# Weight splits recorded one preparation later, attention handed out more often, in a one-core encoder layer

## The chip, the cores and the metric

The kernel runs on one core of one Trainium2 chip. It uses five engines: PE (matrix products; PEld is its loading of stationary operands), DVE and ACT (elementwise work), POOL (here only the issue of DMAs that add) and SP (the issue of all other DMAs). The metric is the time of one execution in device microseconds (us). The kernel before took 2253.76 us, the median of three runs between 2248.48 and 2257.56.

## The reference

The layer is applied to a prompt of 512 tokens and to a sample of 1024 tokens, with the same weights and a model width of 2048. Cut to what matters:

```python
def mixer_layer(x, ...):
    h = rms_norm(x, norm_g)
    z = h @ w_in                      # 2048 -> 5632 columns
    c_val, c_glu, c_gate, q, k, v, a_gate = split(z)
    q, k = rope(q), rope(k)           # 8 query heads, 2 key/value heads of 128
    conv = (silu(layer_norm(depthwise31(c_val * sigmoid(c_glu)) + b)) @ w_pw) * silu(c_gate)
    attn = banded_sink_attention(q, k, v, sink) * silu(a_gate)   # window 128, blocks of 128
    return x + concat([conv, attn]) @ w_out
# the encoder is one such layer and a final rms_norm
```

All of it is float32. A product on PE runs on float32r operands, so each float32 operand is split in two (a rounded high part, made by ACT, and the remainder, made by DVE), and three matmuls (high-high, high-low, low-high) stand for one.

## The kernel before, in words

**Stages.** The sample is projected first, by units. A `Unit` makes two column tiles of 128 for all 1024 tokens over half of the 2048 rows of `w_in`, as a two-by-two block product with seven products in place of eight. So a unit has seven steps of 12 matmuls of 512 columns, 84 in all, and needs four weight operands (made by `make0` to `make3`), one for steps 0 and 1, one for 2 and 3, one for 4 and 5, one for 6. There are 44 units in four stages: 8 convolution units on the first half of the rows, 8 on the second, then 14 units of the remaining columns on the second half, and the same 14 on the first half. Three of the four stages begin with a pair of units whose steps alternate (the second of them has `side` set). Then the prompt is projected by 44 jobs of 48 matmuls (`Job`, line 482; the weight is split again, or its low part is fetched as the units stored it). After that come three tails (`Post`): the sample's first and second 512 tokens, and the prompt. Each is the pointwise product (8 jobs of 24 matmuls) and the output product (16 jobs of 48; the last tail makes it in another form, line 1228).

**The weight splits.** `w_prep(upto)` makes the operands in order up to (not including) number `upto`: ACT copies the raw weight tile into the high half of an `hl` tile (line 350), DVE subtracts for the low half (line 351), and for `make1` to `make3` DVE first forms sums of raw blocks (line 136). There are three `hl` buffers and three `raw` buffers. While step or job with operand `i` is recorded, the kernel before calls `w_prep(i + NHL)` with NHL = 3 behind its first products, so operands up to `i + 2` are made there; a call `w_prep(i + 1)` stands ahead of each step. Each operand made also starts the load of raw tiles up to two numbers ahead.

**What sets the order.** The code records instructions; a scheduler then gives each engine one fixed order, by the order of recording and by priority (weight splits, evacuations and what follows them are recorded as urgent). On the chip every engine goes through its order one by one, and an instruction that waits holds up what is behind it on its engine.

**Evacuation of a unit.** After each step `tap` reads a bank of sums: ACT copies (line 208) or DVE adds the bank to an earlier copy (line 210). Four of the seven taps complete a tile of 128 columns by 512 tokens: the taps of steps 1, 4 and 5 (DVE) and 6 (ACT). On the second half of the rows that a column group sees, POOL then issues a DMA that adds the stored sums of the first half into the tile in place (`add_into`, line 341), and an entry is put in a list, `later`, with the count LANDING = 4. Each recorded step calls `turn_over`, which takes one off each count, and at zero records `done` for the tile behind the DVE and ACT instructions recorded last: the multiplication by the rms factor (lines 739 and 741 with a sigmoid between, 745 for the product with the gate, 754 for gates and values) or the rotation of a query or key (lines 806 to 809), all on DVE. Bank `a` is one running sum over steps 0, 2, 4 and 6, so step 6 cannot start before DVE has read the bank behind step 4. This second half is the convolution units of the second stage (8 units) and all units of the fourth (14): 88 added tiles.

**Lanes.** Work that has no fixed place is put in lanes (convolution taps, line 778; attention; preparations). After each group of three matmuls the code calls `tick(648 ns)`; a lane gets a credit of that time times its rate, and records pieces of work, each with a cost in the code, while its credit is positive. From the start of the prompt's projection the attention lane has the rate RUSH = 1.2. It holds the sample's two groups of 8 blocks, then the 8 heads of `attention_parts` for the first tail, then the prompt's two groups of 4 blocks. Before the first output product of a tail all 8 heads must be there: `until` records the rest of the lane at once, with no products between. The same is done for the prompt's attention ahead of the last tail's preparation. In the code's costs a block of attention is 38.8 us (35.3 at the ends of a sequence), the keys and values of a group are 22 us (11 for the prompt), a head of `attention_parts` is 6 us.

Of the kernel before, what the change touches and what calls it, by code (L numbers as in the profile page):

```python
# [34 lines left out]
NORM = 2  # L35
SOON = 800
PM = 30
RUSH = 1.2
LANDING = 4
LOAD = 4500  # L40
SPREAD = 3
RATES = (0.4, 0.6, 0.3, 1.0)
# [2 lines left out]
NT, NRAW, NHL = 28, 3, 3  # L45
# [40 lines left out]
class Unit:  # L86
# [82 lines left out]
    def product(self, step, late):  # L169
        e, nc = self.e, self.e.nc  # L170
        p, o = OPERAND[step]
        i = self.at[p]
        e.w_prep(i + 1)
        hl = e.hl[i]
        n = BANK[step]
        if step in FRESH:
            self.bank[n] = e.PS(self.tags[n], [W])
        acc = self.bank[n]
        toks = e.T[SUMS[step]]
        for j in range(HALF):  # L180
            for q, (l, r) in enumerate(((0, 0), (0, 1), (1, 0))):
                nc.tensor.matmul(  # L182
                    acc,
                    hl[:, l, o, j, :],
                    toks[j][:, r],
                    start=step in FRESH and j == 0 and q == 0,
                    stop=step in LAST and j == HALF - 1 and q == 2,
                    skip_group_check=True,
                )
            if j == 0:  # L190
                for fn in late:
                    fn()
                e.w_prep(i + NHL)
                e.turn_over()
            e.tick(3 * MM)
        if step in (1, 3, 5, 6):
            e.hl.pop(i)
        for fn in self.after.get(step, ()):
            fn()
        return [lambda: e.urgently(self.tap, step)]  # L200

    def tap(self, step):
# [8 lines left out]
        if step in (1, 4, 5, 6):  # L211
            part, d = self.part[n[0]][n[1]], self.d.pop(n)
            if self.done:

                e.add_into(d, part)
                e.later.append([LANDING, lambda: self.done(n[0], n[1], d)])
            else:
# [53 lines left out]
class Encoder:  # L271
# [182 lines left out]
    def run(self, items):  # L454

        nc = self.nc
        late = []
        for n, item in enumerate(items):
            for x in item:
                for fn in x.before:  # L460
                    fn()
            if isinstance(item[0], Unit):
                for u in item:
                    u.open()
                for step in range(7):
                    for u in item:
                        late = u.product(step, late)
                continue
            while self.later:
                self.turn_over(True)  # L470
            job = item[0]
            job.acc = [self.acc()]
            nk = len(job.ks)
            for q in range(0, nk, 2 * HALF):
                at = job.at + q // (2 * HALF)
                self.w_prep(at + 1)
                hl = self.hl.pop(at)
                for kk in range(2 * HALF):
                    i = q + kk
                    hi, lo = job.rhs(job.ks[i])  # L480
                    for p, (l, r) in enumerate(((0, hi), (0, lo), (1, hi))):
                        nc.tensor.matmul(  # L482
                            job.acc[0],
                            hl[:, l, kk // HALF, kk % HALF, :],
                            r,
                            start=i == 0 and p == 0,
                            stop=i == nk - 1 and p == 2,
                        )
                    if kk == 0:
                        self.w_prep(at + NHL)  # L490
                        self.turn_over()
                    if i in job.ticks:
                        job.ticks[i]()
                    self.tick(3 * MM)
                    if i == 0:
                        for fn in late:
                            fn()
                        late = []
            late = [lambda job=job: self.urgently(job.evac, job.acc)]
        for fn in late:  # L500
            fn()
# [764 lines left out]
def encoder(ctx, tc, a):  # L1266
# [76 lines left out]
    def pace(unit, rate, lane=e.conv):  # L1343
        unit.before.append(lambda: setattr(lane, "rate", rate))
# [53 lines left out]
    pj[0].before.append(attend)  # L1398
    pace(pj[0], RUSH, e.attn)
    pace(pj[0], RATES[3])  # L1400
# [72 lines left out]
```

## Time and profile before

| | |
|---|---|
| Median of the runs | 2253.76 us (2248.48 to 2257.56) |
| The profiled execution: its own time, its span | 2254.38 us, 2252.5 us |
| PE busy, share of the span | 2159.6 us, 96% |
| DVE busy | 1648.9 us, 73% |
| ACT busy | 965.6 us, 43% |
| POOL busy | 77.0 us, 3% |
| DMA | 400.11 MB, 178 GB/s over the span |
| Mean granted clock of PE | 0.98 |

A row of the profile's tables gives the program line, the engine, the operation and the operands, written tile first, without buffer numbers; then the count, the busy time and the mean of one. In a timeline a row begins with its start and its duration in us, and the bracket at its end is the idle time of the engine just before it, with what ended it. Rows of stretches give the stretch's start and end, its length, the busy time and count of each engine (PE, PEld, DVE, ACT, POOL), then the granted clock of PE, the DMA engines' busy share and GB/s. A busy PE is not a PE at its full rate, because matmuls overlap: the full rate is read from the distance of starts.

### The profile page before, as it was taken

The numbers are of one execution on the slowest core, as the hardware profiler recorded it, in microseconds if no ns is written. First come the engines' busy times: TensorE is split into PE (matmuls) and PEld (weight loads), VectorE is DVE, ScalarE is ACT, GpSimd is POOL, SyncE is SP. The second block draws the span as 40 slices with busy tenths as digits, with TensorE's granted clock in tenths as the row PEclk, the third lists the DMA queues.
The fourth block names the chain that finished last, engine by engine and source line by source line (L and its number), as shares of the span: only waits on it lengthen the run. The fifth ranks groups of instructions, "written<-read, shape, count | busy, mean of one in ns | idle before, by whom it ended". The sixth has DMA issues, their size and how long they took to land.

```text
span 2252.5 us, 26360 instructions
## 1 busy us (share of the span) xinstructions
PE 2159.6 (96%) x9510; PEld 1752.0 (78%) x9510; DVE 1648.9 (73%) x2497; ACT 965.6 (43%) x1484; POOL 77.0 (3%) x92
## 2 busy tenths in 40 slices
PE   6999899999999999899999999996999999999998
PEld 5887777888877787688888888884788777888886
DVE  8657788988898999799986688673663775746343
ACT  5465335333443334433444457443352544623232
POOL 0001110000011111000000000000000000000000
PEclk8999999999999999999999999996999999999999
DMA  8968767754576666855444644443542482447342
GB/s 283 321 221 245 203 168 255 263 178 164 196 202 175 157 164 160 262 176 168 141 140 142 201 139 136 149 143 120 186 154 104 153 286 84 163 136 259 103 131 75
DMA packets 207748, 400.11 MB, mean 178 GB/s; under 512 B 18945, under 2 KB 76673, under 8 KB 207617
## 3 DMA queue, kind: packets, MB, share of 16 engines
q1 hardware_dynamic: 194944, 375.35, 49.5%
q0 software_dynamic: 12672, 23.07, 6.4%
q8 instruction: 74, 1.21, 0.2%
q14 instruction: 58, 0.47, 0.1%
HBM read 294.02 MB, written 104.33 MB: 177 GB/s over the span
## 4 chain that ended last, share of the span: by engine, by line
PE 68%; DVE 6%; DMA 5%; issue 2%; ACT 1%; SPq 0%; POOL 0%; ACTq 0%; DVEq 0%; POOLq 0%
PE a L482 19%; PE c L482 10%; PE b L482 9%; PE a L182 9%; PE c L182 4%; PE pv L921 2%; PE s L889 2%; PE b L182 2%; PE a L1228 2%; PE s L1228 2%; DMA raw<-w_in 1%; PE pt L926 1%; DVE hl L351 1%; DVE f L778 1%; DMA u<-q_d 1%
## 5 line engine op out<-in xcount | busy, mean ns | idle before, releaser
L351 DVE TENSOR_TENSOR hl<-raw,hl 128x1024 fp32r<-128x1024 f32 (+1 forms) x323 | 371.8, 1151 | 248.3 <-ACT hl L350 243.4
L350 ACT ACTIVATE hl<-raw 128x1024 fp32r<-128x1024 f32 (+1 forms) x323 | 323.0, 1000 | 537.0 <-PE a L482 110.5
L482 PE MATMUL a<-t,hl 128*128 128x512 f32 x2112 | 511.9, 392 | 0.0
L182 PE MATMUL a<-t,hl 128*128 128x512 f32 x1968 | 480.9, 396 | 30.0 <-DVE g L210 17.9
L182 PEld LDWEIGHTS a<-t,hl 128*128 128x128 f32 x1968 | 374.5, 191 | 116.9 <-DVE g L210 25.1
L482 PEld LDWEIGHTS a<-t,hl 128*128 128x128 f32 x2112 | 393.4, 188 | 78.5
L778 DVE SCALAR_TENSOR_TENSOR f<-f,c_w_dw,f 128x1024 f32<-128x1024 f32 (+1 forms) x464 | 453.4, 1012 | 1.0 <-ACT f L773 1.0
L482 PE MATMUL b<-t,hl 128*128 128x512 f32 x1056 | 260.0, 395 | 10.7 <-ACT t L350 10.4
L482 PE MATMUL c<-t,hl 128*128 128x512 f32 x1056 | 256.2, 392 | 0.1
L182 PE MATMUL c<-t,hl 128*128 128x512 f32 x984 | 240.9, 392 | 9.7 <-ACT t L350 5.7
L482 PEld LDWEIGHTS b<-t,hl 128*128 128x128 f32 x1056 | 197.3, 189 | 56.8 <-ACT t L350 14.3
L482 PEld LDWEIGHTS c<-t,hl 128*128 128x128 f32 x1056 | 196.4, 188 | 39.4 <-DVE hl L351 0.5
L182 PEld LDWEIGHTS c<-t,hl 128*128 128x128 f32 x984 | 185.0, 188 | 51.6 <-ACT t L350 7.0
L182 PE MATMUL b<-t,hl 128*128 128x512 f32 x492 | 118.5, 389 | 0.0
L136 DVE TENSOR_TENSOR raw<-raw,raw 128x512 f32<-128x512 f32 x123 | 84.6, 688 | 38.6 <-DMA raw<-w_in 28.3
L182 PEld LDWEIGHTS b<-t,hl 128*128 128x128 f32 x492 | 92.3, 188 | 19.1
L208 ACT ACTIVATE u<-a 128x512 f32<-128x512 f32 x66 | 39.4, 597 | 91.8 <-PE a L182 86.9
L921 PE MATMUL pv<-a,t 128*128 128x512 f32 x192 | 71.1, 434 | 4.8 <-ACT a L350 3.9
L1228 PE MATMUL a<-hl,t 128*128 128x512 f32 x192 | 74.7, 390 | 0.0
L889 PE MATMUL s<-t,a 128*128 128x384 f32 (+1 forms) x288 | 61.5, 344 | 11.6 <-ACT a L350 10.0
L903 ACT ACTIVATE p<-p,tiny 128x384 f32<-128x384 f32 (+1 forms) x96 | 54.5, 569 | 38.8 <-DVE tiny L900 38.6
L889 PEld LDWEIGHTS s<-t,a 128*128 128x128 f32 x288 | 49.8, 201 | 23.8 <-ACT a L350 14.1
(242 smaller groups left out, 2139.5 us busy)
## 6 DMA issues: line engine op xcount, KB each, us to landing
raw<-w_in SPq DMA_DIRECT2D x169, 512.0 KB, 4.8
raw<-w_out SPq DMA_DIRECT2D x64, 512.0 KB, 3.9
raw<-w_out SPq DMA_DIRECT2D x64, 256.0 KB, 3.3
raw<-w_pw SPq DMA_DIRECT2D x24, 512.0 KB, 3.5
f<-xT_s SPq DMA_DIRECT2D x38, 256.0 KB, 5.9
f<-x_s SPq DMA_DIRECT2D x16, 512.0 KB, 6.1
f<-x_p SPq DMA_DIRECT2D x13, 512.0 KB, 7.2
g<-part_q POOLq DMA_DIRECT2D x24, 256.0 KB, 4.9
```

What stands on the lines that cost most here:

```text
L136: self.e.nc.vector.tensor_tensor(out, x, y, ALU.subtract)
L182: nc.tensor.matmul(acc, hl[:, l, o, j, :], toks[j][:, r], start=step in FRESH and j == 0 and q == 0, stop=step in LAST and j == HALF - 1 a ...
L208: nc.scalar.activation(self.d[n], bank, AF.Copy)
L350: nc.scalar.activation(hi, x, AF.Copy)
L351: nc.vector.tensor_tensor(lo, x, hi.bitcast(F32), ALU.subtract)
L482: nc.tensor.matmul(job.acc[0], hl[:, l, kk // HALF, kk % HALF, :], r, start=i == 0 and p == 0, stop=i == nk - 1 and p == 2,)
L778: nc.vector.scalar_tensor_tensor(t, h[:, j : j + T], w(j), t, ALU.mult, ALU.add)
L889: nc.tensor.matmul(ps[:, 0:n], qs[:, x, h], k[y][:, keys], start=p == 0, stop=p == 2)
L903: nc.scalar.activation(p[:, 0:n], p[:, 0:n], AF.Exp, bias=nm[:, h : h + 1], accum_out=l[:, h : h + 1])
L921: nc.tensor.matmul(pv, v[x][:, vs], pt[:, y], start=i == 0 and p == 0, stop=i == last and p == 2)
L926: nc.tensor.transpose(tp[:, h], p[:, i * P : (i + 1) * P], e.ident)
L1228: nc.tensor.matmul(acc, self.mix[self.KS[i]][:, m, b * P : (b + 1) * P], part[l].rearrange("p a b -> p (a b)"), start=i == 0 and p == 0, s ...
```

## The change

Three things are changed. Weight splits are recorded one operand less far ahead (`NHL - 1` in place of `NHL`), and in units only in every second step (the odd ones for a `side` unit, the even ones for the others). LANDING goes from 4 to 3, so that `done` is recorded one step earlier. RUSH goes from 1.2 to 1.45. The number of matmuls, splits, taps and DMAs is the same; behind line 192 the lines of the changed kernel are two higher.

```diff
-RUSH = 1.2
-LANDING = 4
+RUSH = 1.45
+LANDING = 3
...
@@ Unit.product
             if j == 0:
                 for fn in late:
                     fn()
-                e.w_prep(i + NHL)
+
+                if step % 2 == self.side:
+                    e.w_prep(i + NHL - 1)
                 e.turn_over()
             e.tick(3 * MM)
...
@@ Encoder.run
                     if kk == 0:
-                        self.w_prep(at + NHL)
+                        self.w_prep(at + NHL - 1)
                         self.turn_over()
```

How the order moves is seen at two places. The first is DVE in a query unit of the fourth stage. `g_5675<-a` is the tap of step 4, `g_5654<-c` the tap of step 5, a wait on DMASW is a wait for an added tile; the order before:

```order
L210 TENSOR_TENSOR g_5675<-a_5573,g_5675 128x512 [waits DMAHW3_49,PE_49]
L806 TENSOR_TENSOR u_5694<-u_5599,f_5003 64x512 [waits DMASW0_49]
L807 TENSOR_TENSOR u_5694<-u_5599,f_5003 64x512
L136 TENSOR_TENSOR raw_5584<-raw_5584,raw_5715 128x512 [waits DVE_49]
L808 TENSOR_TENSOR u_5599<-u_5599,f_5002 128x512 [waits DVE_49]
L210 TENSOR_TENSOR g_5654<-c_5650,g_5654 128x512 [waits DMAHW6_49,PE_49]
L809 TENSOR_TENSOR u_5599<-u_5599,u_5694 128x512 [waits DVE_49]
L351 TENSOR_TENSOR hl_5718<-raw_5715,hl_5718 128x1024 [waits Activation_49]
L778 SCALAR_TENSOR_TENSOR f_5610<-f_5485,c_w_dw,f_5610 128x1024
L351 TENSOR_TENSOR hl_5738<-raw_5631,hl_5738 128x1024 [waits PE_49,Activation_49]
L778 SCALAR_TENSOR_TENSOR f_5609<-f_5485,c_w_dw,f_5609 128x1024
L754 TENSOR_TENSOR g_5675<-g_5675,f_1667 128x512 [waits DMASW1_49]
```

Ten rows stand between the tap of step 4 and line 754, which takes the tile after its addition. The same unit on DVE in the changed kernel, from the tap of step 4:

```order
L212 TENSOR_TENSOR g_5670<-a_5571,g_5670 128x512 [waits DMAHW6_49,PE_49]
L136 TENSOR_TENSOR raw_5634<-raw_5634,raw_5732 128x512 [waits DVE_49]
L780 SCALAR_TENSOR_TENSOR f_5567<-f_5449,c_w_dw,f_5567 128x1024
L212 TENSOR_TENSOR u_5655<-c_5651,u_5655 128x512 [waits PE_49]
L353 TENSOR_TENSOR hl_5735<-raw_5732,hl_5735 128x1024 [waits Activation_49]
L756 TENSOR_TENSOR g_5670<-g_5670,f_1661 128x512 [waits DMASW1_49]
L780 SCALAR_TENSOR_TENSOR f_5568<-f_5449,c_w_dw,f_5568 128x1024
L756 TENSOR_TENSOR u_5655<-u_5655,f_1661 128x512 [waits DMASW2_49]
```

Four rows are left between the tap of step 4 and line 756 (754 before), three between the tap of step 5 and its line 756. The weight split `hl` that stood ahead of them (with a wait for PE) comes later, and `done` with its DMA wait has moved up. The tap of step 1 and its rotation stand closer as well: before, 12 rows lie between them, now 4:

```order
L212 TENSOR_TENSOR u_5754<-b_5750,u_5754 128x512 [waits DMAHW4_49,PE_49,Activation_49]
L353 TENSOR_TENSOR hl_5817<-raw_5634,hl_5817 128x512 [waits Activation_49]
L780 SCALAR_TENSOR_TENSOR f_5567<-f_5449,c_w_dw,f_5567 128x1024
L136 TENSOR_TENSOR raw_5876<-raw_5820,raw_5778 128x512 [waits DMAHW7_49,DMAHW1_49,DVE_49]
L136 TENSOR_TENSOR raw_5876<-raw_5820,raw_5876 128x512 [waits DVE_49]
L808 TENSOR_TENSOR u_5822<-u_5754,f_4999 64x512 [waits DMAHW6_49,DMASW4_49]
```

Here line 808 (806 before) waits for the tile that line 212 (210 before) completed, with a split, one convolution tap and two raw sums between.

The second place is PE around the first output product. Before, the last block of the sample's attention (`pt` are transposes, `pv` the product with the values) ends like this, and the output product follows at once:

```order
L921 MATMUL pv_12022<-a_12028,t_1290_9660 128x512 [waits Activation_49]
L921 MATMUL pv_12022<-a_12028,t_1290_9660 128x512 [waits DVE_49]
L921 MATMUL pv_12022<-a_12028,t_1291_9661 128x512
L926 MATMUL pt_12034<-c_ident,p_11989 128x128 [waits PE_49]
L926 MATMUL pt_12034<-c_ident,p_11995 128x128
L926 MATMUL pt_12034<-c_ident,p_12001 128x128
L926 MATMUL pt_12034<-c_ident,p_12007 128x128
L921 MATMUL pv_12022<-a_12039,t_1290_9660 128x512 [waits Activation_49]
L921 MATMUL pv_12022<-a_12039,t_1290_9660 128x512 [waits DVE_49]
L921 MATMUL pv_12022<-a_12039,t_1291_9661 128x512
L482 MATMUL b_12114<-t_1665_12053,hl_11847 128x512 [waits Activation_49]
L482 MATMUL b_12114<-t_1665_12053,hl_11847 128x512 [waits DVE_49]
```

No product of a projection stands between these rows. In the changed kernel the last block of the sample's attention is spread through the prompt's projection (`c` and `a` are its sums, line 484 is 482 before):

```order
L928 MATMUL pt_11653<-c_ident,p_11503 128x128 [waits PE_49]
L928 MATMUL pt_11653<-c_ident,p_11509 128x128
L928 MATMUL pt_11653<-c_ident,p_11529 128x128
L928 MATMUL pt_11653<-c_ident,p_11535 128x128
L484 MATMUL c_11565<-t_909_7018,hl_11472 128x512 x3
L484 MATMUL c_11565<-t_910_7021,hl_11472 128x512 x3
L484 MATMUL c_11565<-t_911_7024,hl_11472 128x512 x3
L484 MATMUL a_11673<-t_886_6915,hl_11621 128x512 x3
L923 MATMUL pv_11630<-a_11658,t_1261_9344 128x512 [waits Activation_49]
L923 MATMUL pv_11630<-a_11658,t_1261_9344 128x512 [waits DVE_49]
L923 MATMUL pv_11630<-a_11658,t_1262_9345 128x512
L484 MATMUL a_11673<-t_887_6918,hl_11621 128x512 x3
```

Between the transposes and the products that need them there are now 12 matmuls of the projection, and the block ends at PE's matmul 6301 in place of 6538.

## The prediction, made before the changed kernel ran

> **What bounds the kernel now.** I read the page first, then stretches cut at the stages, then the timelines where PE waits.
>
> ```profile
> span 2252.5 us, 26360 instructions
> PE 2159.6 (96%) x9510; PEld 1752.0 (78%) x9510; DVE 1648.9 (73%) x2497; ACT 965.6 (43%) x1484; POOL 77.0 (3%) x92
> ```
> ```profile
> 407.17 5.44 PE a L182 x24
> ```
> ```profile
> 180.70:349.70 169.00, 156.63 (x673) 126.91 (x672) 135.46 (x177) 66.68 (x94) 26.93 (x31) 0.98 0.74 203
> 622.60:916.60 294.00, 277.42 (x1194) 225.96 (x1193) 263.25 (x346) 122.35 (x176) 47.97 (x55) 0.98 0.67 178
> 916.60:1528.30 611.70, 608.03 (x2778) 495.96 (x2777) 498.99 (x819) 289.67 (x458) 0.87 (x1) 1.00 0.49 159
> 1528.30:1581.50 53.20, 32.28 (x94) 18.38 (x91) 20.02 (x39) 14.28 (x29) 0.00 (x0) 0.68 0.41 129
> ```
> PE is the bound nearly everywhere. Its full rate is in the chain of waits: 24 matmuls in 5.44 us, so 0.2267 us each and 19.04 us for a unit of 84. By that rate the second stage (8 units, 152.3 us) has lost 16.7 us of its 169.0, and the fourth (14 units, 266.6 us) 27.4 of its 294.0. The prompt's projection, 916.6 to 1528.3, shows PE busy for 608 of 612 us. Then comes a hole: in 53.2 us PE runs 94 matmuls, which need at most 94 x 0.2267 = 21.3 us, and its clock is 0.68. In the fourth stage DVE is busy for 263 of 294 us: there it has next to nothing to spare.
>
> **Part 1: the hole (RUSH).**
>
> ```profile
> 1525.65 2.89 PE L482 MATMUL a<-t,hl 128*128 128x512 f32 x12
> 1528.37 0.60 PE L926 MATMUL pt<-c_ident,p 128*128 128x128 f32 x4
> ...
> 1548.48 1.09 PE L926 MATMUL pt<-c_ident,p 128*128 128x128 f32 x4 [3.88 <-DVE p L911]
> ...
> 1562.23 1.95 PE L482 MATMUL b<-t,hl 128*128 128x512 f32 x3 [6.53 <-ACT t L350]
> ```
> These rows of PE's timeline are what `until` recorded at once: the end of the sample's attention and the 8 heads, with nothing of a projection to put between. The credits say why. 44 jobs of 16 groups and 8 of 8 groups, 0.648 each, give 498 us by the first output product. The sample's attention costs 651 and the 8 heads 48, together 699. At 1.2 the lane has 597, so 102 are left; at 1.45 it has 722, and nothing is. The order bears it out (the last block ends 237 matmuls sooner, among products). What moves into the projection is about 20 us of DVE and 14 of ACT; there DVE is busy for 499 and ACT for 290 of 612 us, so it is covered; without that cover it would cost up to those 20 us. Gain: at least 53.2 - 21.3 = 31.9, at most 36, since transposes and scores are shorter than 0.2267; I take 33, as a wait or two stays.
>
> The prompt's attention is due later. Past the hole 218 us of ticks give 261 at 1.2 against its 318, so it is forced too; at 1.45 it has 23 + 316 = 339 and is through.
>
> ```profile
> PE s L889 <- ACT a L350: 8.6, 4, 4.1
> ```
> That is PE's wait for attention operands between 1580 and 2030 us; I take 6 of the 8.6 (bounds 0 and 8.6). Together 39.
>
> **Part 2: the splits recorded later.** The same splits are made. An `hl` tile is free when its last reader is through, and with three buffers that instant does not move; only the place in DVE's and ACT's order does. What is behind an early split waits with it:
>
> ```profile
> DVE hl L351 <- ACT hl L350: 248.8, 153, 6.6
> PE s L182 <- ACT hl L350: 5.2, 1, 5.2
> ```
> ```profile
> L350 ACT ACTIVATE hl<-raw 128x1024 fp32r<-128x1024 f32 (+1 forms) x323 | 323.0, 1000 | 537.0 <-PE a L482 110.5
> L351 DVE TENSOR_TENSOR hl<-raw,hl 128x1024 fp32r<-128x1024 f32 (+1 forms) x323 | 371.8, 1151 | 248.3 <-ACT hl L350 243.4
> L208 ACT ACTIVATE u<-a 128x512 f32<-128x512 f32 x66 | 39.4, 597 | 91.8 <-PE a L182 86.9
> ```
> The first row is DVE's wait for splits over the span (longest 6.6); PE is not held by it except where DVE is full. Its end is worth nothing by itself, since PE's own wait for a split is the second row alone (the first pair of the fourth stage), which goes: 5 us. In the other direction, a unit's operand must be there 24 matmuls (5.4 us) after the one before; a split is 1.0 us on ACT and 1.15 on DVE (the third row, line 208, is the ACT copy of a tap, 0.6 us, for part 3). That holds, unless DVE is late for another reason; bounds +5 and -5, and I take 0, since four additions of that pair now come close on their taps as in part 3.
>
> **Part 3: `done` closer to the DMA it needs (LANDING and the splits).** This is what the order shows on DVE. Durations are those of a unit before, by the distance of starts:
>
> ```profile
> 723.13 1.22 DVE L351 TENSOR_TENSOR hl<-raw,hl 128x1024 fp32r<-128x1024 f32 x1
> 724.27 0.68 DVE L210 TENSOR_TENSOR g<-a,g 128x512 f32<-128x512 f32 x1
> 724.98 0.69 DVE L806 TENSOR_TENSOR u<-u,f 64x512 f32<-64x512 f32 x1
> 725.68 0.68 DVE L807 TENSOR_TENSOR u<-u,f 64x512 f32<-64x512 f32 x1
> 726.40 0.69 DVE L136 TENSOR_TENSOR raw<-raw,raw 128x512 f32<-128x512 f32 x1
> 727.01 0.68 DVE L808 TENSOR_TENSOR u<-u,f 128x512 f32<-128x512 f32 x1
> 727.61 0.68 DVE L210 TENSOR_TENSOR g<-c,g 128x512 f32<-128x512 f32 x1
> 728.21 0.68 DVE L809 TENSOR_TENSOR u<-u,u 128x512 f32<-128x512 f32 x1
> 728.81 1.22 DVE L351 TENSOR_TENSOR hl<-raw,hl 128x1024 fp32r<-128x1024 f32 x1
> 729.94 1.28 DVE L778 SCALAR_TENSOR_TENSOR f<-f,c_w_dw,f 128x1024 f32<-128x1024 f32 x1
> 731.14 1.22 DVE L351 TENSOR_TENSOR hl<-raw,hl 128x1024 fp32r<-128x1024 f32 x1
> 732.27 1.28 DVE L778 SCALAR_TENSOR_TENSOR f<-f,c_w_dw,f 128x1024 f32<-128x1024 f32 x1
> 733.47 0.68 DVE L754 TENSOR_TENSOR g<-g,f 128x512 f32<-128x512 f32 x1
> ```
> ```profile
> 728.70 0.86 POOL L341 DMA_DIRECT2D g<-part_q  x1 [2.27 <-DVE g L210]
> ```
> ```profile
> g<-part_q POOLq DMA_DIRECT2D x1, 256.0 KB, 4.1
> g<-part_q POOLq DMA_DIRECT2D x1, 256.0 KB, 4.8
> g<-part_q POOLq DMA_DIRECT2D x1, 256.0 KB, 5.8
> u<-part_q POOLq DMA_DIRECT2D x1, 256.0 KB, 5.4
> ```
> ```profile
> DMA to landing us min/median/max: 3.8/5.2/9.5
> ```
> A split takes 1.14, a convolution tap 1.20, the two half rotations 0.70 each, every other row 0.6. POOL begins 0.41 us after a tap's end (728.29 to 728.70), and the four additions of one unit (787 to 799 us) land 4.1, 4.8, 5.8 and 5.4 later. Before, the tap of step 4 ends at 724.95 and line 754 begins at 733.47, 8.5 us on: the 4.5 needed are covered. Now the rows between them:
>
> - Tap of step 4 from 0 to 0.65; raw sum, convolution tap and the tap of step 5 to 3.05; a split to 4.2. Its tile is there at 0.65 + 0.41 + 4.1 = 5.15: DVE waits 0.95.
> - Line 754 to 5.75, a tap to 6.95. The tile of step 5 is there at 3.05 + 0.41 + 4.8 = 8.25: 1.3 more. Then 0.6 and a split, 10.0.
> - The tile of step 6: PE may start the step at 0.75, ends at 3.5 (5.1 at half clock), ACT copies to 4.2 to 5.8, POOL and landing 6.2: there at 10.4 to 12.0, wait 0.4 to 2.0, I take 1.2. Rotation (2.6) and the tap of step 1 to 14.45; split, tap and two raw sums to 17.45.
> - That tile is there at 14.45 + 0.41 + 5.4 = 20.25: 2.8. Rotation, raw sum and a split: 24.6, and the next unit's tap of step 4.
>
> So a unit has 18.3 us of DVE work and 6.3 of waits, 24.6 us, where PE needs 19.04: the stage becomes DVE's, and PE waits behind step 4 for bank `a`. The trace before shows once what that looks like:
>
> ```profile
> 254.87 0.69 DVE L739 TENSOR_TENSOR u<-u,f 128x512 f32<-128x512 f32 x1 [3.44 <-DMA u<-part_conv]
> ```
> ```profile
> 264.39 7.70 PE L182 MATMUL a<-t,hl 128*128 128x512 f32 x24 [4.58 <-DVE g L210]
> ```
> One addition late by 3.44 us, and PE stood still for 4.58 soon after, then ran 24 matmuls in 7.70 in place of 5.6, at half clock.
>
> ```profile
> 708.70:871.30 162.60, 156.92 (x673) 127.90 (x672) 0.98 0.62 159
> ```
> The eight query units took 162.6 us, 20.3 each. Now 8 x 24.6 = 197, less 3 that PE's lead at their start absorbs (step 5, 12 matmuls, lies between the tap's end of step 4 and step 6): +31. The stage's other six units took 294.0 - 162.6 = 131.4, 21.9 each. Four of them (keys and values, and the last two) have 16 to 19 us of DVE work by the same durations and get the same waits, about 23.4 each: +6, an estimate. In the second stage a unit has four or five convolution taps, 16.6 to 17.8 us of DVE work by the same durations; three of its four additions are read 2.6 to 3.5 us of work after their taps, and the waits by the same sum are 5.4 (1.8, 0.8, 2.8): 22 to 23.2 us a unit against 169.0 / 8 = 21.1, with seven units so placed and the loss of 254 us kept: +14. Sum +51. Bounds: with every landing at 3.8 the waits are 2.6 a unit, and the sum is +15; nothing below that, as no row shows a shorter landing. With half of them at 7 it is +90.
>
> The Trainium skill has a rule that speaks the other way: by "DMA: Bandwidth & Descriptors", section "Anatomy of one DMA — SWDGE (gpsimd) path", a DMA from POOL takes about 2.0 us plus its bytes at 436 KB/us, so an estimate of 2.6 us for 256 KB. By that estimate every tile is there within the 3 us of work between, and part 3 costs nothing. The rows disagree, at 3.8 at the least; the page's sum is for a plain transfer.
>
> **Sum.** 2254.4 (the profiled execution) - 39 + 0 + 51 = 2266; the median shown is 0.6 below that execution, which I leave out.
>
> **Rivals.** 0.5% of this kernel, 11 us, is about what a measurement tells from no change.
>
> *A. Landings fall into the work.* With DVE-bound units the DMA engines (0.67 busy) have less to do per us, and if additions land in 3.8 or sooner, part 3 is +15 or less: 2254 - 39 + 15 = 2230, without any wait 2215. It decides where the waits are below 4 us a unit. For it: half of the landings lie below the median of 5.2, the first of a unit at 4.1. Against it: the fourth tile of a unit has 3.0 us of work before it and needs 5.8. This is the faster side.
>
> *B. The hole's work costs PE in the projection.* With 1.45 a block of attention has 17% less of PE's time between its steps. If PE waits there for ACT and DVE as often as the 8.6 us above in the prompt's blocks, sixteen blocks give back 17 to 34 of the 39: 2283 to 2300. Against it: PE's busy share in that stretch was 0.99 at 1.2.
>
> *C. The two parts cancel*, with waits near 4.5 us a unit: 2243 to 2254.
>
> **Chances.** The forecast as worked, 2254 to 2285: 0.5, of it 0.15 within 0.5%. A 0.25, faster. B 0.15, slower. C 0.1, of it 0.08 within. So faster 0.25 + 0.02, within 0.5% 0.23, slower 0.5. From 2225 to 2300 some 2 in 10 are left out, below by landings without waits, above by B on top of late landings.
>
> **What would show it.** Right: DVE waits at lines 741, 747, 756 and 808 for added tiles, some 1.5 us for each of 88; the query units at 24 us; PE waiting for DVE line 212; no stretch after the prompt's projection with a clock of 0.68. Wrong: those DVE waits below 60 us in sum, or PE waits for attention in the projection.

## The result and the profile after

The changed kernel takes 2264.81 us, the median of six runs (2261.66 to 2273.49), against 2252.91 for the kernel before in six runs (2248.48 to 2257.56): a ratio of 1.0058, 95% interval 1.0036 to 1.0080. It is slower by 12 us, or 0.6%, and close to the 2266 forecast. The sum is right; several of its terms are not.

The page of the changed kernel, then its stretches: second stage, fourth stage, the eight query units in it, the prompt's projection, and the 64 us behind that, where the hole was.

```profile
span 2263.4 us, 26350 instructions
PE 2158.1 (95%) x9510; PEld 1764.4 (78%) x9510; DVE 1650.3 (73%) x2497; ACT 968.8 (43%) x1488; POOL 76.9 (3%) x92
```
```profile
180.90:370.70 189.80, 164.89 (x674) 131.87 (x673) 138.67 (x177) 67.78 (x97) 26.70 (x31) 0.94 0.67 178
...
648.10:974.90 326.80, 288.37 (x1194) 232.06 (x1193) 264.85 (x344) 125.16 (x180) 47.86 (x55) 0.95 0.63 160
739.50:926.70 187.20, 164.64 (x681) 132.39 (x680) 152.07 (x195) 56.76 (x80) 26.93 (x31) 0.95 0.56 135
974.90:1550.40 575.50, 569.15 (x2635) 470.45 (x2634) 482.42 (x810) 286.95 (x462) 0.88 (x1) 1.00 0.49 160
1550.40:1614.00 63.60, 63.60 (x291) 52.90 (x290) 47.80 (x76) 28.70 (x46) 0.00 (x0) 1.00 0.76 253
```

The second stage was 169.0 us and is 189.8 (+21); the third, between these two rows, was 272.9 and is 277.4 (+4.5); the fourth was 294.0 and is 326.8 (+33), of which the query units have +24.6 (162.6 to 187.2). The units end at 974.9 in place of 916.6: 58 us lost. From there to the end it was 1335.9 and is 1288.5: 47 us gained. The last row has no hole: PE is busy throughout, at full clock.

Where the units' 58 us went is read from the line that issues the adding DMAs (343, 341 before). Its list of who waited, with the us in sum and the times:

```profile
  DVE g L756: 20.4, 14
  DVE u L756: 18.6, 13
  DVE u L747: 18.5, 5
  DVE u L808: 10.3, 10
  DVE g L741: 10.3, 7
  DVE g L808: 6.6, 6
  DVE u L741: 6.3, 5
  DVE g L747: 2.6, 1
```
```profile
DMA to landing us min/median/max: 3.8/4.6/8.8
```

A landing is the time from POOL's issue until the sum stands in the tile. DVE waits 93.6 us in 61 places for added tiles. Before, the same list came to 10.4:

```profile
  DVE u L739: 6.5, 4
  DVE g L754: 2.0, 1
  DVE u L754: 1.2, 1
  DVE u L806: 0.7, 2
```

One query unit on DVE, from the tap of step 4 to the next unit's:

```profile
807.31 0.68 DVE L212 TENSOR_TENSOR g<-a,g 128x512 f32<-128x512 f32 x1
...
812.48 0.69 DVE L756 TENSOR_TENSOR g<-g,f 128x512 f32<-128x512 f32 x1 [0.96 <-DMA g<-part_q]
...
815.11 0.69 DVE L756 TENSOR_TENSOR u<-u,f 128x512 f32<-128x512 f32 x1 [0.74 <-DMA u<-part_q]
...
818.60 0.69 DVE L808 TENSOR_TENSOR g<-g,f 64x512 f32<-64x512 f32 x1 [1.66 <-DMA g<-part_q]
...
821.35 0.68 DVE L212 TENSOR_TENSOR u<-b,u 128x512 f32<-128x512 f32 x1
...
826.25 0.69 DVE L808 TENSOR_TENSOR u<-u,f 64x512 f32<-64x512 f32 x1 [1.09 <-DMA u<-part_q]
...
830.74 0.68 DVE L212 TENSOR_TENSOR g<-a,g 128x512 f32<-128x512 f32 x1
```

The unit lasts 23.43 us, 4.45 of it these four waits. In all eight query units DVE waits 34.3 us for added tiles, 4.3 a unit, and by their row above it is busy for 152.1: together 186.4 of the 187.2 us, so this stretch is DVE's. What PE waits for, over the span (in sum, times, longest), and the same two waits in the kernel before:

```profile
PE a L182 <- DVE g L212: 27.5, 15, 4.3
PE c L182 <- ACT g L210: 21.5, 6, 6.3
```
```profile
PE a L182 <- DVE g L210: 17.9, 14, 4.6
PE c L182 <- ACT g L208: 1.5, 2, 0.8
```

The first wait, 17.9 before, has the cause that the prediction named. The second, 1.5 before, was not foreseen. Timelines of ACT, PE and DVE show it in the second stage:

```profile
291.66 0.63 ACT L742 ACTIVATE g<-g 128x512 f32<-128x512 f32 x1 [6.09 <-DVE g L741]
292.19 0.58 ACT L210 ACTIVATE g<-c 128x512 f32<-128x512 f32 x1
```
```profile
292.82 4.40 PE L182 MATMUL c<-t,hl 128*128 128x512 f32 x12 [3.18 <-ACT g L210]
```
```profile
290.93 0.69 DVE L741 TENSOR_TENSOR g<-g,f 128x512 f32<-128x512 f32 x1 [2.05 <-DMA g<-part_conv]
```

`done` of a convolution unit is a multiplication on DVE, a sigmoid on ACT (line 742), and the product on DVE. ACT stands at the sigmoid until DVE has the added tile (the last row: DVE's multiplication waits 2.05 us for it), and behind the sigmoid in ACT's order is the copy that empties bank `c` (line 210). So PE, which needs the bank, waits for a landing through two engines.

A stand of PE can also cost clock. This is the stretch around the PE row above:

```profile
292.40:295.80 3.40, 2.98 (x7) 2.40 (x8) 3.40 (x5) 1.32 (x2) 0.00 (x0) 0.50 0.00 0
```

PE stood from 289.64 to 292.82, for 3.18 us, and from 292.4 the clock was 0.50 for 3.4 us. In the second to fourth stages of the changed kernel 14 stands of PE, of 1.97 to 6.31 us, have such a stretch of 3.4 or 6.8 us around their ends; the shorter stands, and one of 2.45, have none. At the stage rows' clocks (0.94 and 0.95 after, 0.98 in both before), the second and fourth stages have 0.12 x 189.8 + 0.10 x 326.8 = 55 us at half clock, against 0.04 x (169.0 + 294.0) = 19 before. Each us at half clock costs at most half a us, so this is at most some 18 of the 58 us. PE's listed waits in the units come to 86.8 us against 49.0 before, 38 more, so that the two together make up 56 of the 58.

### The profile page after: what moved, and what is told of

Same layout as the page of the kernel before. It is cut to its first block, busy times and chain, and to the rows that moved or that the text cites. A ratio compares the mean times of both kernels' runs of the same rounds, so it can differ in the third digit from the quotient of the medians.

```text
span 2263.4 us, 26350 instructions
## 1 busy us (share of the span) xinstructions
PE 2158.1 (95%) x9510; PEld 1764.4 (78%) x9510; DVE 1650.3 (73%) x2497; ACT 968.8 (43%) x1488; POOL 76.9 (3%) x92
## 4 chain that ended last, share of the span: by engine, by line
PE 58%; issue 14%; DVE 5%; DMA 4%; POOL 2%; ACT 1%; SPq 0%; POOLq 0%; ACTq 0%; DVEq 0%
PE a L484 20%; PE b L484 10%; PE c L484 10%; PE a L182 3%; PE pv L923 2%; PE a L1230 2%; PE s L1230 2%; DVE f L780 2%; PE s L891 2%; PE c L182 2%; DMA raw<-w_in 1%; PE pt L928 1%; DVE hl L353 1%; PE pv L1230 1%; PE b L1230 1%
## 5 line engine op out<-in xcount | busy, mean ns | idle before, releaser
L182 PE MATMUL c<-t,hl 128*128 128x512 f32 x984 | 252.2, 405 | 29.7 <-ACT g L210 21.5
L484 PE MATMUL b<-t,hl 128*128 128x512 f32 x1056 | 253.6, 392 | 1.9 <-DVE a L1083 1.9
L484 PE MATMUL c<-t,hl 128*128 128x512 f32 x1056 | 251.9, 391 | 0.0
L182 PEld LDWEIGHTS c<-t,hl 128*128 128x128 f32 x984 | 192.1, 196 | 75.6 <-ACT g L210 24.0
L484 PEld LDWEIGHTS c<-t,hl 128*128 128x128 f32 x1056 | 197.2, 188 | 40.1 <-DVE a L1083 0.3
L182 PE MATMUL b<-t,hl 128*128 128x512 f32 x492 | 119.4, 391 | 0.0
L210 ACT ACTIVATE u<-a 128x512 f32<-128x512 f32 x76 | 45.2, 595 | 96.0 <-PE a L182 94.0
L352 ACT ACTIVATE a<-pt 128x512 fp32r<-128x512 f32 x64 | 38.1, 596 | 79.6 <-PE pt L928 79.5
L353 DVE TENSOR_TENSOR a<-pt,a 128x512 fp32r<-128x512 f32 x64 | 44.0, 687 | 27.4 <-ACT a L352 26.8
L210 ACT ACTIVATE g<-a 128x512 f32<-128x512 f32 x47 | 27.9, 595 | 78.4 <-PE a L182 76.8
```

Of the source, the lines that this page charges most:

```text
L182: nc.tensor.matmul(acc, hl[:, l, o, j, :], toks[j][:, r], start=step in FRESH and j == 0 and q == 0, stop=step in LAST and j == HALF - 1 a ...
L210: nc.scalar.activation(self.d[n], bank, AF.Copy)
L352: nc.scalar.activation(hi, x, AF.Copy)
L353: nc.vector.tensor_tensor(lo, x, hi.bitcast(F32), ALU.subtract)
L484: nc.tensor.matmul(job.acc[0], hl[:, l, kk // HALF, kk % HALF, :], r, start=i == 0 and p == 0, stop=i == nk - 1 and p == 2,)
```

## The experiments

The theory to be tested, T: the taking instruction waits only where DVE's work between the tap and it is shorter than the landing; LANDING and the later splits each use up part of that distance, so apart they cost little and together much; RUSH is worth its 39 us by itself. The main rivals: LANDING alone (L) or the later splits alone (P, K) make the loss; the hole's work comes back as waits in the projection (B). This table collects what was measured. The units' end and the waits for added tiles come from each kernel's trace. Later stands for later in units and jobs.

| kernel | splits in units | LANDING | RUSH | us (ratio, 95%) | units end | waits for added tiles |
|---|---|---|---|---|---|---|
| before | early | 4 | 1.2 | 2252.91 | 916.6 | 10.4 |
| e1_rush | early | 4 | 1.45 | 2216.18 (0.9834, 0.9820 to 0.9849) | 914.3 | 11.8 |
| e2_landing3 | early | 3 | 1.2 | 2263.45 (1.0042, 1.0027 to 1.0056) | 922.7 | 38.8 |
| e3_prep | later | 4 | 1.2 | 2257.76 (1.0019, 1.0009 to 1.0029) | 928.3 | 51.1 |
| e4_after_l4 | later | 4 | 1.45 | 2221.16 (0.9854, 0.9839 to 0.9868) | 928.5 | 48.3 |
| changed kernel | later | 3 | 1.45 | 2264.81 (1.0058, 1.0036 to 1.0080) | 974.9 | 93.6 |
| e6_after_l5 | later | 5 | 1.45 | 2209.41 (0.9810, 0.9791 to 0.9828) | 913.7 | 17.6 |
| e12_after_l6 | later | 6 | 1.45 | 2207.50 (0.9794, 0.9776 to 0.9812) | 913.6 | 1.5 |
| e5_jobs | early, later in jobs | 4 | 1.45 | 2207.84 (0.9809, 0.9794 to 0.9823) | 918.9 | 11.0 |
| e8_jobs_l5 | early, later in jobs | 5 | 1.45 | 2199.26 (0.9767, 0.9751 to 0.9784) | 904.6 | 5.6 |
| e9_jobs_l6 | early, later in jobs | 6 | 1.45 | 2194.76 (0.9754, 0.9737 to 0.9770) | 900.5 | 3.9 |
| e10_rush16 | early, later in jobs | 5 | 1.6 | 2208.10 (0.9810, 0.9794 to 0.9826) | 904.8 | 4.4 |
| e7_noadd | later, no additions | 3 | 1.45 | 2177.73 (0.9670, 0.9656 to 0.9684) | 889.8 | none |
| e11_quarter | later, a quarter added | 3 | 1.45 | 2205.53 (0.9797, 0.9778 to 0.9816) | 909.0 | 33.7 |

**RUSH alone (e1_rush).**

```diff
-RUSH = 1.2
+RUSH = 1.45
```

> The kernel before with the attention handed out at 1.45 in place of 1.2, nothing else. Theory T (the three parts hardly touch one another; the hole closes and the tails gain as in the changed kernel, and the projection pays nothing): the stretch from the end of the units to the end falls by 47 us as it did in the changed kernel (1335.9 to 1288.5), the units stay as before, so 2252.9 - 47 = 2206 (2198 to 2214). Rival B (the hole's work costs PE in the prompt's projection, and something of the later splits in the jobs hides it in the changed kernel): 17 to 34 us come back, 2223 to 2240, with PE's waits in the projection for attention operands.

Measured 2216.18, 37 us faster. Its projection and the place of the hole; then PE's longest wait in the projection, which is 0.2 us in the kernel before; then the stretch from the units' end to the end:

```profile
914.30:1495.90 581.60, 574.01 (x2635) 467.22 (x2634) 480.24 (x806) 287.63 (x464) 0.87 (x1) 1.00 0.49 158
1495.90:1560.00 64.10, 64.10 (x293) 53.05 (x292) 50.66 (x81) 29.46 (x48) 0.00 (x0) 1.00 0.76 255
```
```profile
PE s L889 <- ACT a L350: 6.0, 4, 2.6
```
```profile
914.30:2213.10 1298.80, 1278.03 (x5793) 1045.47 (x5791) 884.14 (x1493) 570.08 (x910) 0.87 (x1) 0.99 0.49 159
```

The hole is gone, and the last stretch falls by 37 us, from 1335.9 to 1298.8. T forecast 2206 (to 2214), ten less, and misses: it had counted the changed kernel's whole 47 us to RUSH. Against PE's full rate, by the distances of its matmuls' starts (0.2267 us each, less for narrow ones), the projection loses 20.1 us in place of 13.8, the place of the hole 0.3 in place of 36.4, and the rest 13.3 in place of 20.6: +6 - 36 - 7. (The rate taken for narrow matmuls moves each of these estimates by some us, the differences hardly.) So B occurs in small, at 6 us, and as a forecast of the time it falls. The other 10 us are taken up with e3_prep and e5_jobs.

**LANDING alone (e2_landing3) and the later splits alone (e3_prep).**

```diff
-LANDING = 4
+LANDING = 3
```

> The kernel before with LANDING 3 in place of 4, splits and attention as before. On DVE's order the median of the work between a tap that completes an added tile and the instruction that takes that tile is 8.3 us before, 6.5 us here and 3.5 us in the changed kernel, against landings of 3.8 to 9.5 us. Theory T (a wait begins only where that work is shorter than the landing, so LANDING and the later splits cost little apart and much together): DVE's waits for added tiles are some 15 us in sum in place of 10 before and 94 in the changed kernel, and the time is 2250 to 2266. Rival L (LANDING alone brings the waits): all the 58 us of the units, 2305 to 2315.

```diff
-                e.w_prep(i + NHL)
+
+                if step % 2 == self.side:
+                    e.w_prep(i + NHL - 1)
...
-                        self.w_prep(at + NHL)
+                        self.w_prep(at + NHL - 1)
```

> The kernel before with the weight splits recorded later, in units and in jobs; LANDING 4 and attention at 1.2 as before. The median work between tap and taking instruction is 6.5 us here as well. Theory T: waits for added tiles of some 16 us in sum, 2250 to 2268. Rival P (the later splits themselves bring the loss, since splits come when DVE is late and PE waits for them): most of the 58 us, 2295 to 2315, with PE's waits for hl tiles well above the 5.2 us of before and with the waits for added tiles still small.

Both times fall in T's ranges: 2263.45 (+10) and 2257.76 (+4). L and P fall. The fourth stage of e2 and of e3:

```profile
618.60:922.70 304.10, 277.92 (x1194) 225.56 (x1193) 261.59 (x343) 122.69 (x175) 47.86 (x55) 0.98 0.65 171
```
```profile
624.20:928.30 304.10, 280.28 (x1194) 227.90 (x1193) 263.08 (x343) 123.75 (x178) 48.01 (x55) 0.97 0.66 171
```

Each edit costs the fourth stage 10 us; the two together cost it 33. The waits for added tiles are 38.8 and 51.1 us, where T expected some 15 and 16: single landings take up to 9, above the median of 6.5 us of work between. Against the 10.4 us of before, 28 and 41 us more of DVE waits cost the units only 6 and 12 us, and 83 us more cost 58. That the first waits fall into time in which DVE was ahead of PE is the likely reading. (With units as before, three kernels end them at 914.3, 916.6 and 918.9, so some 2 us either way is their scatter.) e3 also shows something that was not asked: behind the units it is 7.4 us shorter than before (2256.8 - 928.3 = 1328.5 against 1335.9), while e2 is 3.1 us longer there.

**The changed kernel with LANDING 4 again (e4_after_l4).**

```diff
-LANDING = 3
+LANDING = 4
```

> The changed kernel with LANDING 4 again (splits later, attention at 1.45). Theory T: the waits for added tiles fall from 94 us to about 16, with them PE's waits for bank c behind ACT (21.5 us), whose copies stand behind sigmoids that wait for DVE, and the units come back to within 10 us of before: 2206 to 2218, faster than both kernels. Rival P: the loss is the later splits', and the time stays within 10 us of 2265.

Measured 2221.16: one number gives back 44 us. T has the direction, but its time was three us short, the units end 12 us behind those of before and not within 10, and the waits are 48.3, not 16. P falls. PE's waits for bank `c` behind ACT's copy of `g` are gone from its list, and the fourth stage takes 299.0 us.

**Without the additions (e7_noadd), and with a quarter of them (e11_quarter).**

```diff
-        self.nc.gpsimd.dma_start(dst, src, accum_op=ALU.add)
+        pass
```

> The changed kernel without the 88 adding DMAs: the stored sums of the first half are left out of the result, all else is computed as before. Theory T (the loss of the units is the wait for landings and what follows from it, the copies on ACT behind sigmoids and PE's waits for banks): the units end 45 to 60 us sooner than in the changed kernel, at 915 to 930, and the time is 2205 to 2220. Rival P (the loss is the later splits' and the denser order on DVE, with the landings merely in the same place): the time stays above 2250.

```diff
-        self.nc.gpsimd.dma_start(dst, src, accum_op=ALU.add)
+        self.nc.gpsimd.dma_start(dst[:, : W // 4], src[:, : W // 4], accum_op=ALU.add)
```

> The changed kernel with the adding DMAs on the first 128 of the 512 columns of each tile, 64 KB in place of 256; the sums of the other 384 columns lack the first half of the rows. It prices the landing. If a landing is mostly bytes, the least falls from 3.8 to about 2 us and the median from 4.6 to 2.5; then the 3 us of work between cover it, the waits for added tiles fall from 94 to some 10 us, and the time comes to that without additions, 2178 to 2190. If it is mostly a fixed part, the landings stay above 3.3 us, 60 us or more of waits are left, and the time is 2230 to 2260.

Without additions the time is 2177.73 and the units end at 889.8, 85 us sooner than in the changed kernel and 27 sooner than before. P falls. T had the direction, but the gain is 27 us beyond its range: the kernel before, too, pays for its additions. Second and fourth stages without additions:

```profile
180.70:335.70 155.00, 153.09 (x674) 125.82 (x673) 137.47 (x177) 69.14 (x97) 0.00 (x0) 1.00 0.50 168
609.20:889.80 280.60, 273.17 (x1194) 224.28 (x1193) 263.30 (x345) 124.68 (x180) 0.00 (x0) 0.98 0.41 138
```

The second stage is at 155.0 us, against 152.3 for PE at its full rate. The run takes away the waits and also the traffic (DMA share 0.41 in place of 0.63), and DVE's order shifts a little with it (2374 of its 2497 instructions keep their order), so it bounds what the additions cost rather than what waiting alone costs. With a quarter of the bytes, the same issues have this landing:

```profile
DMA to landing us min/median/max: 2.5/2.9/6.9
```

Neither forecast holds: 33.7 us of waits, 2205.53, between the two. From 64 to 256 KB the least landing goes from 2.5 to 3.8 and the median from 2.9 to 4.6, which is 148 and 113 KB/us and a fixed part of 2.1 to 2.3 us, if the time goes in a straight line with the bytes; two sizes cannot show that.

**The later splits in the jobs alone (e5_jobs).**

```diff
-RUSH = 1.2
+RUSH = 1.45
...
-                        self.w_prep(at + NHL)
+                        self.w_prep(at + NHL - 1)
```

> The kernel before with attention at 1.45 and the later splits in the jobs alone; units and LANDING as before. From the units' end to the end of the span the runs with later splits were shorter by 7.4 us (before 1335.9, splits later 1328.5) and by 7.6 us (attention alone 1298.8, changed kernel with LANDING 4 1291.2). Theory T (that gain is the jobs' edit, the loss is the units' edit): the units as with attention alone (914.3), the rest at 1291, so 2216.2 - 7.5 = 2209 (2204 to 2213). Rival U (the gain comes from the units' edit, which moves other work past the units' end): no gain, 2216.

Measured 2207.84, 8 us under RUSH alone (the two intervals just touch). In the profiles the stretch behind the units is 1293.2 in place of 1298.8. So the gain behind the units is the jobs' edit, and the loss in the units is the units' edit; U falls as far as these intervals go. By the same measure the projection loses 15.8 us in place of 20.1, so most of this gain lies there. Whether it is what attention at 1.45 had cost is not shown, since e3_prep gains as much behind the units with attention at 1.2. No single wait carries it; which ones do stays open. (The execution profiled here was the longest of the four, 2213.89 us, so the units' end at 918.9 is probably late by some us.)

**More distance: LANDING 5 and 6, with splits later or early in the units.**

```diff
-LANDING = 3
+LANDING = 5
```

> The changed kernel with LANDING 5. The median work between a tap and the instruction that takes the added tile is 7.4 us, 6.5 us with LANDING 4, 3.5 us in the changed kernel. Theory T (waits for added tiles follow from that work alone): waits of some 20 us in sum in place of 48 with LANDING 4, and 2221.2 less 5 to 12: 2209 to 2216. Rival K (what is left of the units' loss is the later splits', whatever LANDING is): 2219 to 2224.

Measured 2209.41, 17.6 us of waits: as T says. K falls.

```diff
-LANDING = 4
+LANDING = 5
```

The next kernel is e5_jobs with that edit.

> The kernel before with attention at 1.45, the later splits in the jobs alone, and LANDING 5. Work between tap and taking instruction has a median of 10.7 us. Theory T: the 10 us of waits for added tiles that are left with LANDING 4 fall to some 4, and 0 to 5 us are gained over the same kernel with LANDING 4: 2204 to 2209. Rival H (tiles held one step longer delay the taps that need a free buffer, and the convolution that reads the gate product): 2212 or more.

Measured 2199.26, better than T's range; H falls. The second stage falls from 170.5 us (e5_jobs) to 154.7, though only 6.1 us of waits for its added tiles were there to go. PE's waits account for most of it: there it had stood 9.5 us for bank `a` behind DVE, with a clock of 0.97 over the stage; now it has no such wait, and the clock is 1.00. e10_rush16 below, with the same units, has 155.3 us there as well.

```profile
180.10:334.80 154.70, 153.19 (x673) 125.89 (x672) 131.96 (x174) 66.42 (x93) 26.28 (x30) 1.00 0.81 220
608.70:904.60 295.90, 276.11 (x1194) 222.61 (x1193) 263.38 (x345) 121.20 (x175) 47.93 (x55) 0.99 0.67 174
```

The fourth stage stays at 296 although its waits for tiles are few. There DVE waits for raw weight tiles (first row), as it did before (11.2), and less so with LANDING 6 (second), the next run:

```profile
DVE raw L136 <- DMA raw<-w_in: 13.0, 10, 2.6
```
```profile
DVE raw L136 <- DMA raw<-w_in: 1.7, 3, 1.0
```

> As the kernel with LANDING 5, attention at 1.45 and later splits in the jobs alone (2199.3 us), with LANDING 6: median work between tap and taking instruction 13.6 us in place of 10.7. Theory T: 5.6 us of waits for added tiles are left with LANDING 5, on PE's path at most 3, so there is no more to gain: 2196 to 2202. Rival H (finished tiles that come a step later are missed by the convolution, the preparations and the buffers): 2203 or more.

Measured 2194.76, 0.9754 of the kernel before (0.9737 to 0.9770): faster than both kernels of this case, and the lowest median with all the work done, though its interval overlaps that of LANDING 5. T's range holds, H falls, and T's reason holds only in part: the fourth stage went to 281.0 us, as without additions, and the second back to 163.3.

```profile
180.00:343.30 163.30, 155.71 (x674) 126.50 (x673) 129.84 (x172) 66.11 (x93) 26.29 (x30) 0.99 0.76 207
619.50:900.50 281.00, 272.60 (x1194) 222.61 (x1193) 261.42 (x342) 121.90 (x173) 47.35 (x55) 0.99 0.69 182
```

The changed kernel with LANDING 6:

> The changed kernel with LANDING 6 (splits later in units and jobs, attention at 1.45). The median work between tap and taking instruction is 10.7 us. In the fourth stage of the kernel before, and of the one with LANDING 5 and early splits in the units, DVE also waits 11 to 13 us for raw tiles of w_in ahead of the raw sums; no such wait is left in the changed kernel. Theory T (later splits in the units cost nothing once the work covers the landings, and take those raw waits away): waits for added tiles under 10 us, the units end at 890 to 902, and the time is 2184 to 2196. Rival K (the later splits in the units have a cost of their own, whatever LANDING is): 2200 to 2212, as with LANDING 5.

Measured 2207.50: T falls here, K holds. The waits for added tiles are 1.5 us, yet the units end at 913.6, and the waits for raw tiles, which T said would be gone, are there:

```profile
DVE raw L136 <- DMA raw<-w_in: 14.1, 10, 2.1
```

So with the landings covered the later splits in the units still cost 13 us there against early ones (913.6 and 900.5; 9 us by the ratios of the whole times), by a way that is not settled: the raw waits appear in e8 with early splits as well, and in e7, without additions, the fourth stage has none of them and takes 280.6 us with the later splits.

**RUSH 1.6 (e10_rush16), on e8_jobs_l5.**

```diff
-RUSH = 1.45
+RUSH = 1.6
```

> The same kernel with LANDING 5 and attention at 1.6 in place of 1.45. Theory T: at 1.45 nothing is left of the sample's attention at the first output product and nothing of the prompt's at the last tail, so more gives no more: 2197 to 2202. Rival B (blocks handed out more often have less of PE's time between their steps, and PE waits for ACT and DVE in the projection, 28 us of loss behind the units as it is): 2204 to 2212.

Measured 2208.10, 9 us slower. The units are unchanged (904.8); behind them PE waits, over 904 to 1560 us, for attention operands:

```profile
PE s L889 <- ACT a L350: 9.4, 7, 3.5
```

Over the whole rest it is 15.1 us, against 4.5 with 1.45. B, wrong at 1.45, is right at 1.6: more credit only brings waits.

## Why the prediction came out right

**Part 1, the hole: right, by mechanism and size.** The hole closes, no stretch behind the projection has a clock of 0.68, and RUSH alone is worth 37 us of the 39 forecast: 36 at the hole (33 forecast), 7 behind it (6 forecast), less 6 in the projection, which the prediction had called covered. That is rival B at a third of its lower price; one of the two "wrong" signs, waits of PE for attention in the projection, is thus there in e1_rush, with 6.0 us. In the changed kernel the projection loses 14.0 us, as before, with the jobs' later splits.

**Part 2, the splits recorded later: 0 forecast, two halves of opposite sign.** Alone, the units lose 11.7 us (916.6 to 928.3), and behind them 7.4 are gained, which was not foreseen; the sum of +4 lay within the bounds of 5. That is in part luck: the 11.7 come with 51.1 us of waits for added tiles, which the prediction prices in part 3, and with the landings covered (LANDING 6) the later splits cost the units 13, outside those bounds. The detail was wrong that the pair's 5.2 us wait would go: in the changed kernel it is 3.4, and 2.0 more for DVE's half of a split.

**Part 3, `done` closer to its DMA: right in mechanism, its terms off both ways.** The waits stand at lines 741, 747, 756 and 808, query units last 23.4 us (24.6 forecast), and PE waits for DVE at line 212. The term of the query units was sized at +31 and measured +24.6. The step that failed there is the wait for the fourth tile, 2.8 us by 5.8 from the tap's end to the landing (0.41 and 5.4): in the unit shown the tap of step 1 begins at 821.35, ends 0.6 later, and its tile is waited for until 826.25, 4.3 us after that; the wait is 1.09. Landings came sooner (median 4.6 in place of 5.2), with DMA share in the query units down from 0.62 to 0.56, which is what rival A argued, in part. So the waits were 94 us and not the some 130 of the signs.

Here the total was lucky. The query units have 4.3 us of waits each in place of 6.3, and by the prediction's own sum waits near 4.5 were rival C, 2243 to 2254. By that sum 4.3 gives 8 x (18.3 + 4.3) - 3 - 162.6 = +15. The other 10 us come from two more terms that were off: DVE's work is 152.1 / 8 = 19.0 us a unit in place of 18.3, and nothing is seen of the 3 us that PE's lead was to absorb.

The second stage was sized at +14, the upper end of what its own 22 to 23.2 us a unit give (6 to 15), and measured +21, though its waits are about 4 us a unit in place of 5.4, because the sum followed DVE alone. The way over the sigmoid and ACT's copy to bank `c` was missing, and so was the half clock after PE's longer stands, which the quoted matmuls at 7.70 us had shown. The other six units of the fourth stage have +8.2 (forecast +6), the third stage +4.5 (forecast nothing).

Summed: -39 + 51 = +12 forecast; measured -47.4 + 58.3 = +11 in the traces, +12 in the medians. The likeness of the totals owes much to chance: behind the units 10 us were gained beside RUSH (1298.8 to 1288.5), 6 to 8 of them by the jobs' later splits, which part 2 put at nothing, and the loss in the units was 7 larger than its sum.

That LANDING and the splits must be priced together is shown: alone they cost 10 and 4 us, together, beside RUSH, 2264.81 - 2216.18 = 49. The prediction was spared an error there only because it counted the rows left by both.

## What to carry to other kernels

A fixed engine order holds a reserve between an asynchronous transfer and the instruction that takes its result. Count that reserve in us of work and compare it with the transfer's landing, and price together all edits that draw on it: each may be nearly free and the pair dear. Then follow every instruction that stands behind the wait on each engine in turn, since the bottleneck may wait through two of them and pay again in clock.

## What the runs showed of the hardware

- An adding DMA from POOL lands in some 2.1 to 2.3 us plus its bytes at 113 to 148 KB/us, an estimate from two sizes (64 KB: 2.5 at the least, median 2.9; 256 KB: 3.8 and 4.6). By the Trainium skill, "DMA: Bandwidth & Descriptors", section "Anatomy of one DMA — SWDGE (gpsimd) path", a DMA on that path takes about 2.0 us plus bytes at 436 KB/us; it has no term for an addition. The fixed part agrees; the rate for additions is a quarter to a third of that, and the measurement decides.
- PE's clock fell to 0.50 for 3.4 us around the end of a stand of only 3.18 us, and the shortest stand with such a stretch around its end was 1.97 us. The Trainium skill, "TensorE: Matmul & The Clock Gate", section "Part 1: The HAM clock gate", gives at least one idle window of about 3.4 us as the condition; the length of the slow stretch agrees with that window, these stands were shorter.
- Waits for the weight loads of 512 KB (up to 17.3 us in the fourth stage, in e6_after_l5) come and go with the order alone: 11.2 before, 0.5 in the changed kernel, 13.0 and 1.7 with LANDING 5 and 6 and early splits. What decides it was not found.
